# Weight slabs split ahead of time, and filling steps dealt out by another table

## The chip, the cores and the metric

The kernel runs on one NeuronCore of a Trainium2 chip. Its engines are named as in the profile: PE (matrix multiplication; PEld is its loading of weights), DVE (VectorE), ACT (ScalarE), POOL (GpSimd) and SP, which only issues transfers. Each engine takes its instructions in a fixed order. The metric is the device time of one execution in microseconds (us); the time before is the median of three runs.

## The reference

A two-layer decoder over one sequence of 1024 tokens with 1024 features. Layer 0 mixes tokens by differential attention, layer 1 by forgetting attention, and each is followed by a gated MLP; a layer norm stands after each of the four parts. Only layer 1's attention is touched:

```python
def forgetting_attention(x, w_in, b_f, w_o):
    q, k, v, f_logit = jnp.split(x @ w_in, [H * d, 2 * H * d, 3 * H * d], axis=-1)
    ...
    log_f = jax.nn.log_sigmoid((f_logit + b_f).astype(jnp.float32))
    c = jnp.cumsum(log_f, axis=1).transpose(0, 2, 1)
    ...
        s = (jnp.einsum('bhqd,bhkd->bhqk', qb, k).astype(jnp.float32) * scale
             + cb[..., :, None] - c[..., None, :])
        p = masked_softmax(s, causal_mask(start, Q_BLOCK, S)).astype(v.dtype)
        o = jnp.einsum('bhqk,bhkd->bqhd', p, v)
    ...
    return sweep_query_blocks(block, S, Q_BLOCK) @ w_o
```

There are 16 heads of 64 features.

## The kernel before

**Numbers in two parts.** Every operand of a dense product is split into a high part and a rest (`split`, line 90): ACT copies the source into the high part's tile, rounded, and DVE subtracts that from the source into the low part's tile. A dense product is then three matmuls (`mm3`, line 100): high with high, high with low, low with high. Because all operations go through such helpers, many instructions of the profile have a helper's line: L93 and L95 are the two halves of a split, L104, L109 and L110 the three matmuls.

**Layer 1's attention, in order of time.**

1. `all_values` (line 430) projects all values. It runs 64 slots (two groups of features, four pairs of token tiles, eight tiles of the contraction), each of two `mm3`, six matmuls. The list `at` hangs other work on a slot: transposes of the layer's input, splits of the value weights, the forget gates, and the splits of the first pair's two weight slabs at slots 36 and 42. Results are split and written to DRAM (`vd`).
2. `first_pair` (line 417) projects q (slab 0) and k (slab 1) of the first pair of heads, in two column halves c of 512 tokens, then loads that pair's values (`load_v`) and cumulated gates (`load_c`).
3. The loop over eight pairs of heads in `attention` (line 782). A pair has 16 jobs: head 0 with query tiles 0 to 3, head 1 with the same, head 0 with tiles 4 to 7, head 1 with these. A job (`fox_scores`) forms the scores of 128 queries with all earlier keys (two matmuls a chunk, L591 and L592), their maximum on DVE (L599), the exponential on ACT one job later (L767), and the division by the sum on DVE one job after that (L770, L771). When a group of four jobs is done, `Values` transposes the probabilities on PE two key tiles a job (L1619), splits them from PSUM (L93, L95, tag `pt`, a ring of three tiles) and multiplies them with v one job later (L1645, L1646).

**Filling.** While a pair's jobs run, the next pair's q and k are projected in between, so that PE has work while DVE and ACT do the softmax. This is `project` (line 485): 32 steps of one `mm3` each, eight for k's first half, eight for its second, then q's two. Each group of eight accumulates into one of four PSUM banks (tag `m`), which the transposes and the products with v use too. Step 0 fetches k's slab and step 8 makes q's slab ready; step 24 makes the k slab of the pair after ready, which step 16 fetched. `ahead` (line 339) issues a fetch into one of two staging tiles (`wst`), `ready` (line 344) splits the staged slab into `wh` and `wl` (three buffers each, also used for some of the probabilities).

**The dealing.** How many steps follow each job is set in `attention`: a job has a weight, for layer 1 its number of key tiles plus 2, that is 3, 4, 5, 6, 3, 4, 5, 6, 7, 8, 9, 10, 7, 8, 9, 10, sum 104; after each job, steps are run until the share of steps done is the share of weights passed. The first pair runs 8 steps ahead of its jobs, and the last pair's filling is the output projection. The order in which instructions stand on each engine is laid out from this program order, by priority, when the kernel is built, so neighbours may change places.

**Slabs.** For layer 1, `slabs[3 p]` is the q weight of pair p, `slabs[3 p + 1]` its k weight, each 128 x 1024 numbers of 4 bytes, 512 KB. From 24 on stand the output projection's.

Of the kernel before, what the change touches and what calls it, by code (L numbers as in the profile page):

```python
# [9 lines left out]
F32 = mybir.dt.float32  # L10
F32R = mybir.dt.float32r
# [8 lines left out]
P = 128  # L20
# [3 lines left out]
NP = 8  # L24
# [14 lines left out]
LAG, VLAG, W_C = 1, 0, 2  # L39
# [14 lines left out]
T_ST, N_R, N_A = 2, 4, 6  # L54
X0_A, X0_B, X1 = 2, 2.5, 13
W_V, FRAC = 1, 0
V_T, V_W, V_LD = 5, 8, 12
TT1 = 3


class Trunk:
# [276 lines left out]

    def ahead(self, i):

        if i < len(self.slabs):
            self.stage[i] = self.fetch(self.slabs[i])

    def ready(self, i):
        if i < len(self.slabs):
            self.w[i] = self.cut(self.stage.pop(i))

    def first_loads(self, pos):
# [68 lines left out]
    def first_pair(self, t):  # L417

        self.all_values()
        for c in range(2):  # L420
            for s in range(2):
                if c:
                    self.ready(4) if s else self.ahead(4)
                ps = self.mbank()
                self.dense(ps, *self.w[s], c)
                self.result(1, s, c, ps, None, t)
        self.load_v(0, t)
        self.load_c(0, t)

    def all_values(self):  # L430

        nc = self.nc
        self.vd = [self.dr.tile([P, KT, 4, 2, P], F32, name=f"vd{g}") for g in range(2)]
        own = lambda: self.qtile(0)
        high, low = [partial(self.wp.tile, [P, 1024], F32R, tag=t, name=t + "v") for t in ("wh", "wl")]
        other = partial(self.tmp, F32R, self.pp, "p")  # L440
        homes = ((own,) * 4 + (high, low) * 2, (other,) * 4 + (high,) + (own,) * 3)
        w, stage = {}, {}

        def cut(g, kt):
            if kt % 2 == 0:
                stage[g] = self.fetch(self.i["wv1"][g, kt // 2])
            hl = homes[g][kt]()
            w[g, kt] = hl[:, :512], hl[:, 512:]
            self.split(*w[g, kt], stage[g][:, kt % 2 * 512:kt % 2 * 512 + 512])

        at = [[] for _ in range(64)]
        for kt in range(KT):
            cut(0, kt)
            at[V_T + 2 * kt].append(partial(self.transposes, self.acc, 1, (kt,), True))
            at[V_W + 3 * kt].append(partial(cut, 1, kt))
        at[25] += [partial(self.gate_logits, 1), self.forget_gates]
        for s in range(2):
            at[36 + 6 * s].append(lambda s=s: self.w.update({s: self.weight(self.slabs[s])}))
        at[48].append(self.forget_sums)
        n = 0  # L460
        for g in range(2):
            for t0 in range(0, 8, 2):
                ps = [self.mbank() for _ in range(2)]
                for kt in range(KT):
                    for fn in at[n]:
                        fn()
                    n += 1
                    for j in range(2):
                        self.mm3(ps[j], *self.x_lhs(kt, t0 + j), *w[g, kt], kt == 0, kt == KT - 1)
                for j in range(2):  # L470
                    out = self.tmp(F32R)
                    parts = out.rearrange("p (a b d) -> p a b d", a=4, b=4)
                    self.split(parts[:, :, 0::3], parts[:, :, 1:3], ps[j].rearrange("p (a h d) -> p a h d", a=4, h=2))
                    nc.sync.dma_start(self.vd[g][:, t0 + j], out.bitcast(F32).rearrange("p (a h d) -> p a h d", a=4, h=2))

    def x_lhs(self, kt, tt):
        ts = slice(tt % 4 * P, tt % 4 * P + P)
        return self.xh[kt, tt // 4][:, ts], self.xl[kt, tt // 4][:, ts]
# [303 lines left out]
    def attention(self, l):  # L782

        nc = self.nc
        self.od = self.dr.tile([NP, P, 1024], F32, name=f"od{l}")
        tiles = lambda p: [self.qtile((p + l) % 2) for _ in range(7)] + (
            [self.lp.tile([P, 1024], F32R, tag="lg", name=self.nm("kl"))] if l else [])
        self.slabs = [self.i[f"w{l}"][s * NP + p] if s < 3 - l else None for p in range(NP) for s in range(3)]  # L790
        self.slabs += [self.i[f"wo{l}"][k] for k in range(8)]
        self.w, self.stage, self.queue = {}, {}, []
        self.ofs, self.fill = {}, None
        if l == 1:
            for h in range(2):
                for t in self.qz[h]:
                    nc.gpsimd.memset(t[64:66, :].bitcast(F32), 1.0)
            self.gate_logits(0)
        cur = tiles(0)
        self.first_pair(cur) if l else self.first_pair_rotary(cur)  # L800
        live, values = [], []
        for p in range(NP):
            nxt = tiles(p + 1) if p < NP - 1 else None
            if nxt is not None:
                self.fill, n = self.project(l, p + 1, nxt), 32 if l else 48
            else:
                self.fill, n = self.out_early(l), 64
            jobs = (self.diff_jobs if l == 0 else self.fox_jobs)(p, cur)
            done = 0
            if p == 0:  # L810
                for done in range(1, (EARLY if l else EARLY0) + 1):
                    self.step()
            total, acc, base = sum(j[0] + 1 + W_C for j in jobs) - (W_V * 12 if l == 0 else 0), 0, done

            def steps(goal):
                nonlocal done
                while done < min(goal - 0.5, n):
                    self.step()
                    done += 1

            for job in jobs:
                live, values = self.tick(live, values, job)
                w = job[0] + 1 + W_C - (W_V * self.coming(values) if l == 0 else 0)
                acc += w
                goal = base + (n - base) * acc / total
                steps(done + (goal - done) * FRAC)
                values = self.tock(values)
                steps(goal)
            while done < n:
                self.step()  # L830
                done += 1
            next(self.fill, None)
            cur = nxt
        self.fill, n = self.out_late(l), 12
        while live or values:
            live, values = self.tick(live, values, None)
            values = self.tock(values)
            for _ in range(min(n, T_ST)):
                self.step()
                n -= 1  # L840
        for _ in range(n):
            self.step()
        self.load_o(7, self.ofs[NP - 1])
        for _ in self.fill:
            self.pulse()
# [848 lines left out]
class Norm:  # L1694
# [19 lines left out]
    def tiles(self, t0, n=1):  # L1714
        k = self.k
        return (t0, [k.small(tag="nm") for _ in range(n)],
                *[k.small(n, f"n{j}", 4 if n == 1 else 1) for j in range(3)])
# [120 lines left out]
```

## Time and profile before

| what | us |
|---|---|
| median of three runs | 2409.92 (2409.3 to 2410.89) |
| the profiled execution | 2413.51 |
| its span, first to last instruction | 2410.8 |
| values of layer 1 projected | about 1192 to 1280 |
| first pair projected | 1280 to 1302 |
| seven pairs with a filling projection | about 1302 to 1620 |
| one pair in the middle | 50.0 |

Durations come from the profiled execution. In a table by stretches of time, "x" is a count of instructions, PEclk the share of full TensorE clock that was granted, then the mean busy share of the 16 DMA engines and the rate in GB/s. A line of the waits names who waited, for whose instruction, us in total, times, and the longest. A timeline line has start, duration, engine, line, operation, and what it writes and reads. Groups of instructions end in "xcount | busy us, mean ns", and DMA lines in count, size and median us from issue to landing.

### The profile page before, as it was taken

How to read it: one execution, taken by the hardware profiler on the slowest of the kernel's cores; microseconds unless marked ns; L12 is line 12 of the kernel's file. 1: busy time of each engine (PE TensorE's matmuls, PEld its weight loads, DVE VectorE, ACT ScalarE, POOL GpSimd, SP SyncE). 2: the span in 40 equal slices, each digit the busy share in tenths (PEclk: the TensorE clock that was granted, in tenths of full speed). 3: DMA queues.
4: the chain of work that ended last, by engine and by line, in shares of the span. 5: the costliest groups of instructions: out<-in, count | busy, mean ns of one | idle time of the engine just before them, and what ended most of it. 6: DMA issues, size and time to landing. Idle time of an engine off the chain costs nothing. (4 is left out here: it accounts for less than half of the span.)

```text
span 2410.8 us, 33786 instructions
## 1 busy us (share of the span) xinstructions
PE 2389.0 (99%) x11627; PEld 1981.5 (82%) x11627; DVE 1905.6 (79%) x3740; ACT 1259.6 (52%) x2381; POOL 199.8 (8%) x396
## 2 busy tenths in 40 slices
PE   9999999999999999999999999999999999999998
PEld 7888888778888888888888888888888888888886
DVE  5888888889987877777833888889899887777768
ACT  4656666556544445544523555666465444445434
POOL 2111111010000110100100100101010001110000
PEclk9999999999999999999999999999999999999999
DMA  6223333521433557866334333345223335559672
GB/s 185 67 78 96 88 86 108 188 90 61 171 118 120 128 135 209 250 224 212 131 136 136 86 82 88 91 113 178 90 81 139 123 118 131 132 144 314 197 227 104
DMA packets 159275, 329.02 MB, mean 136 GB/s; under 512 B 21328, under 2 KB 44880, under 8 KB 159104
## 3 DMA queue, kind: packets, MB, share of 16 engines
q1 hardware_dynamic: 147904, 305.83, 39.1%
q0 software_dynamic: 10912, 20.98, 5.4%
q8 instruction: 91, 1.49, 0.2%
q14 instruction: 80, 0.66, 0.1%
q10 hardware_dynamic: 288, 0.07, 0.0%
HBM read 202.60 MB, written 90.64 MB: 122 GB/s over the span
## 5 line engine op out<-in xcount | busy, mean ns | idle before, releaser
L104 PE MATMUL m<-xh,wh 128*128 128x512 f32 x640 | 260.2, 407 | 0.1
L104 PE MATMUL m<-xh,wo 128*128 128x512 f32 x656 | 255.7, 390 | 0.0
L109 PE MATMUL m<-xl,wo 128*128 128x512 f32 x656 | 255.6, 390 | 0.0
L110 PE MATMUL m<-xh,wo 128*128 128x512 f32 x656 | 255.2, 389 | 0.0
L110 PE MATMUL m<-xh,wl 128*128 128x512 f32 x640 | 252.3, 394 | 0.0
L109 PE MATMUL m<-xl,wh 128*128 128x512 f32 x640 | 251.0, 392 | 0.0
L599 DVE CUSTOM_DVE_ANT_0 s<-s,mask 128x384 f32<-128x384 f32 (+7 forms) x256 | 194.2, 760 | 26.6 <-PE s L592 25.8
L93 ACT ACTIVATE wo<-wg 128x512 fp32r<-128x512 f32 (+1 forms) x168 | 102.2, 609 | 168.6 <-PE m L110 141.7
L93 ACT ACTIVATE pt<-m 128x512 fp32r<-128x512 f32 (+3 forms) x285 | 131.5, 491 | 101.6 <-PE m L1619 96.1
L95 DVE TENSOR_TENSOR pt<-m,pt 128x512 fp32r<-128x512 f32 (+3 forms) x285 | 153.8, 557 | 26.3 <-ACT pt L93 24.5
L583 POOL CAST qz<-q 64x128 fp32r<-64x128 f32 x256 | 94.7, 373 | 820.0 <-PE s L592 710.8
L93 ACT ACTIVATE wo<-t 128x512 fp32r<-128x512 f32 x132 | 83.5, 632 | 126.8 <-PE m L110 81.0
L110 PEld LDWEIGHTS m<-xh,wo 128*128 128x128 f32 x656 | 123.1, 188 | 25.6
L104 PEld LDWEIGHTS m<-xh,wo 128*128 128x128 f32 x656 | 123.3, 188 | 24.9 <-ACT p L1312 0.2
L109 PEld LDWEIGHTS m<-xl,wo 128*128 128x128 f32 x656 | 123.3, 188 | 24.3
L110 PEld LDWEIGHTS m<-xh,wl 128*128 128x128 f32 x640 | 120.2, 188 | 26.0 <-DVE wl L95 0.8
L104 PEld LDWEIGHTS m<-xh,wh 128*128 128x128 f32 x640 | 120.5, 188 | 21.1 <-DVE pt L95 1.2
L591 PE MATMUL s<-q,q 128*128 128x512 f32 (+4 forms) x384 | 134.8, 353 | 1.8 <-ACT wst L637 1.6
L95 DVE TENSOR_TENSOR wo<-wg,wo 128x512 fp32r<-128x512 f32 (+1 forms) x168 | 110.5, 659 | 32.8 <-ACT wo L93 32.1
L109 PEld LDWEIGHTS m<-xl,wh 128*128 128x128 f32 x640 | 120.8, 189 | 18.9
L95 DVE TENSOR_TENSOR wo<-t,wo 128x512 fp32r<-128x512 f32 x132 | 90.7, 688 | 48.7 <-ACT wo L93 48.5
L104 PE MATMUL m<-q,wo 128*128 128x512 f32 x328 | 128.6, 392 | 0.0
(416 smaller groups left out, 6528.8 us busy)
## 6 DMA issues: line engine op xcount, KB each, us to landing
wb<-in_wd SPq DMA_DIRECT2D x142, 256.0 KB, 5.2
t<-in_wi SPq DMA_DIRECT2D x44, 512.0 KB, 4.5
ha<-ad SPq DMA_DIRECT2D x86, 256.0 KB, 5.3
wg<-in_wi SPq DMA_DIRECT2D x42, 512.0 KB, 4.0
ad<-t SPq DMA_DIRECT2D x40, 512.0 KB, 2.6
wst<-in_w SPq DMA_DIRECT2D x38, 512.0 KB, 3.6
ha<-sd SPq DMA_DIRECT2D x66, 256.0 KB, 3.9
q<-q SPq DMA_DIRECT2D x128, 128.0 KB, 2.3
```

The source lines that it names most:

```text
L93: self.high = nc.scalar.activation(hi, src, AF.Copy, scale=1.0 if scale is None else scale)
L95: self.low = nc.vector.tensor_tensor(lo, src, hi.bitcast(F32), op=ALU.subtract)
L104: last = mm(out, wh, xh, start=start, stop=False)
L109: mm(out, wh, xl, start=False, stop=False)
L110: mm(out, wl, xh, start=False, stop=stop)
L583: nc.gpsimd.tensor_copy(qz[r:r + 64, :], q[r:r + 64, qt * P:qt * P + P])
L591: nc.tensor.matmul(sb[:, ks], q[:, qt * P:qt * P + P], kd[:, ks], start=True, stop=False)
L599: self.nc.vector.tensor_tensor_reduce(sb[:, :ln], sb[:, :ln], self.mask[:, 1024 - ln:], 1.0, BIG, ALU.add, ALU.min, mn)
```

## The change

Twelve slabs, q and k of the pairs 2 to 7, are fetched and split during the projection of the values: the fetch of number m hangs on slot 3 + 5 m, and the split (`keep`) three slots later. `keep` splits into two tiles of the ring `pt` and writes both parts to DRAM through POOL's queue. `ahead` then does nothing for such a slab, and `ready` loads the two parts from DRAM into `wh` and `wl` instead of splitting. The first pair is projected k first, with both halves, and the loads of gates and values stand between k and q; the slots of its two slabs are swapped. For layer 1's pairs 0 to 6 the weights of the 16 jobs are taken from SHARE, sum 321.

```diff
+SHARE = (13, 27, 21, 9, 6, 19, 20, 8, 32, 30, 14, 15, 39, 37, 15, 16)
+V_T, V_W, V_LD, W_P = 5, 8, 12, 3
...
     def ahead(self, i):
-        if i < len(self.slabs):
+        if i < len(self.slabs) and i not in self.parts:
             self.stage[i] = self.fetch(self.slabs[i])
     def ready(self, i):
-        if i < len(self.slabs):
+        if i in self.parts:
+            self.w[i] = [self.wp.tile([P, 1024], F32R, tag=t, name=self.nm(t)) for t in ("wh", "wl")]
+            for t, part in zip(self.w[i], self.parts.pop(i)):
+                self.nc.sync.dma_start(t.bitcast(F32), part)
+        elif i < len(self.slabs):
             self.w[i] = self.cut(self.stage.pop(i))
...
     def first_pair(self, t):
         self.all_values()
-        for c in range(2):
-            for s in range(2):
-                if c:
-                    self.ready(4) if s else self.ahead(4)
+        for s in (1, 0):
+            for c in range(2):
+                if s == 0:
+                    self.ready(4) if c else self.ahead(4)
                 ps = self.mbank()
                 self.dense(ps, *self.w[s], c)
                 self.result(1, s, c, ps, None, t)
-        self.load_v(0, t)
-        self.load_c(0, t)
+            if s:
+                self.load_c(0, t)
+                self.load_v(0, t)
...
         for s in range(2):
-            at[36 + 6 * s].append(lambda s=s: self.w.update({s: self.weight(self.slabs[s])}))
+            at[42 - 6 * s].append(lambda s=s: self.w.update({s: self.weight(self.slabs[s])}))
         at[48].append(self.forget_sums)
+        for m in range(2 * NP - 4):
+            i = 3 * (2 + m // 2) + (1 - m % 2)
+            at[W_P + 5 * m].append(partial(self.ahead, i))
+            at[W_P + 5 * m + 3].append(partial(self.keep, i))
...
+    def keep(self, i):
+        hl = [self.tt.tile([P, 1024], F32R, tag="pt", name=self.nm("wk")) for _ in range(2)]
+        self.split(*hl, self.stage.pop(i))
+        self.parts[i] = [self.dr.tile([P, 1024], F32, name=self.nm("wk")) for _ in range(2)]
+        for part, t in zip(self.parts[i], hl):
+            self.nc.gpsimd.dma_start(part, t.bitcast(F32))
...
-            total, acc, base = sum(j[0] + 1 + W_C for j in jobs) - (W_V * 12 if l == 0 else 0), 0, done
+            even = l == 1 and p < NP - 1
+            total, acc, base = sum(SHARE) if even else sum(j[0] + 1 + W_C for j in jobs) - (W_V * 12 if l == 0 else 0), 0, done
...
-            for job in jobs:
+            for m, job in enumerate(jobs):
                 live, values = self.tick(live, values, job)
-                w = job[0] + 1 + W_C - (W_V * self.coming(values) if l == 0 else 0)
+                w = SHARE[m] if even else job[0] + 1 + W_C - (W_V * self.coming(values) if l == 0 else 0)
                 acc += w
                 goal = base + (n - base) * acc / total
```

More of the change, by code (lines that the diff above doesn't have):

```diff
@@ L56 @@
 W_V, FRAC = 1, 0
-V_T, V_W, V_LD = 5, 8, 12
+SHARE = (13, 27, 21, 9, 6, 19, 20, 8, 32, 30, 14, 15, 39, 37, 15, 16)
+V_T, V_W, V_LD, W_P = 5, 8, 12, 3
 TT1 = 3
@@ L791, in attention @@
         self.slabs += [self.i[f"wo{l}"][k] for k in range(8)]
-        self.w, self.stage, self.queue = {}, {}, []
+        self.w, self.stage, self.parts, self.queue = {}, {}, {}, []
         self.ofs, self.fill = {}, None
```

## The prediction

> **What bounds the kernel now.** I read the page first, then the table by stretches of time (the windows), the waits, and the timeline where they pointed.
>
> ```profile
> PE 2389.0 (99%) x11627; PEld 1981.5 (82%) x11627; DVE 1905.6 (79%) x3740; ACT 1259.6 (52%) x2381; POOL 199.8 (8%) x396
> core 0: us, PE busy (x) PEld busy (x) DVE busy (x) ACT busy (x) POOL busy (x), PEclk, DMA share, GB/s
> 1192.00:1280.00 88.00, 88.00 (x405) 71.37 (x403) 30.01 (x54) 20.68 (x36) 0.38 (x1) 1.00 0.40 141
> 1280.00:1302.00 22.00, 22.00 (x99) 18.22 (x98) 4.53 (x6) 3.73 (x6) 1.05 (x4) 1.00 0.57 172
> 1302.00:1320.00 18.00, 17.29 (x85) 13.61 (x84) 9.54 (x32) 8.12 (x23) 2.26 (x8) 1.00 0.66 175
> 1393.67:1443.67 50.00, 49.67 (x265) 40.74 (x264) 40.70 (x100) 29.42 (x66) 4.78 (x16) 1.00 0.33 91
> ```
>
> PE is the bound, at full clock (PEclk 1.00). The rows after the page's are the stages that the change touches, all in layer 1: the projection of the values (88 us), the first pair's projection (22 us), the start of the pairs, and one whole pair, which takes 50.00 us and repeats. VectorE (DVE) has 30.01 of 88 us of work in the values stage and 40.70 of 50 in a pair: the first has room, the second little.
>
> "PE busy" does not tell whether PE waits, because a matmul's bar covers its pipeline. I take the distance from start to start:
>
> ```profile
> 1291.78 0.39 PE L104 MATMUL m<-xh,wh 128*128 128x512 f32 x1
> 1292.01 0.39 PE L109 MATMUL m<-xl,wh 128*128 128x512 f32 x1
> 1292.24 0.39 PE L110 MATMUL m<-xh,wl 128*128 128x512 f32 x1
> 1292.46 0.39 PE L104 MATMUL m<-xh,wh 128*128 128x512 f32 x1
> ```
>
> One filling step (three matmuls) takes 1292.46 - 1291.78 = 0.68 us where nothing is waited for. Now the waits of PE's weight loads, first over all the pairs with a filling projection (1302 to 1620 us), then in the two halves of one pair:
>
> ```profile
> PEld m L1646 <- DVE pt L95: 9.7, 30, 0.4
> PEld m L1645 <- ACT pt L93: 7.3, 24, 0.8
> PEld m L1645 <- issue: 1.5, 4, 0.4
> ...
> PEld m L1646 <- DVE pt L95: 1.7, 5, 0.4
> PEld m L1645 <- ACT pt L93: 1.1, 4, 0.4
> PEld m L1645 <- issue: 0.4, 1, 0.4
> ...
> PEld m L104 <- DVE q L95: 0.2, 1, 0.2
> ```
>
> So 18.5 us are waited in seven pairs, nearly all of it by the products (L1645, L1646) for the split of transposed probabilities on ACT and DVE. In one pair it is 3.2 us in the first half (rows four to six) and 0.2 in the second (the last row). The halves are jobs 0 to 8 and jobs 9 to 15; they begin at these score matmuls:
>
> ```profile
> 1393.67 0.22 PE L591 MATMUL s<-q,q 128*128 128x128 f32 x1
> 1418.21 0.40 PE L591 MATMUL s<-q,q 128*128 128x512 f32 x1
> ...
> 1393.67:1418.21 24.54, 24.21 (x131) 19.05 (x130) 20.68 (x59) 15.20 (x38) 2.59 (x9) 1.00 0.28 80
> 1418.21:1443.67 25.46, 25.46 (x135) 21.69 (x134) 20.02 (x41) 14.22 (x28) 2.19 (x7) 1.00 0.39 101
> ...
> 1393.67:1418.21 24.54, 5.25 (x13) 2.46 (x13) 1.00 0.28 80
> 1418.21:1443.67 25.46, 7.85 (x19) 3.58 (x19) 1.00 0.39 101
> ```
>
> The last two rows count line L104, one a step: 13 steps in the first half, 19 in the second. DVE has as much to do in both (20.68, 20.02 us), in many more instructions (59 against 41), so PE runs out of cover in the first half and never in the second.
>
> **The change part by part.**
>
> *The dealing.* With the old weights the jobs 0 to 8 get 43 of 104 shares of 32 steps, 13.2, as counted. With SHARE they get 155 of 321, 15.5. So 2.2 steps, 2.2 x 0.68 = 1.5 us of PE work, move from the half without waits to the half with them. Inside the half it is uneven: jobs 1, 2, 5, 6 and 8 gain 4.1 steps together, jobs 3, 4 and 7 fall from 4.6 to 2.3.
>
> *The splits that leave the pairs.*
>
> ```profile
> L95 DVE TENSOR_TENSOR wl<-wst,wh 128x1024 fp32r<-128x1024 f32 x8 | 9.6, 1206 | 0.0
> L93 ACT ACTIVATE wh<-wst 128x1024 fp32r<-128x1024 f32 x8 | 8.5, 1059 | 1.0 <-PE m L109 1.0
> ...
> 1397.51 1.20 DVE L95 TENSOR_TENSOR wl<-wst,wh 128x1024 fp32r<-128x1024 f32 x1
> 1426.30 1.21 DVE L95 TENSOR_TENSOR wl<-wst,wh 128x1024 fp32r<-128x1024 f32 x1
> ```
>
> Each pair has two, 1.21 us on DVE and 1.06 on ACT each. The one at 1426.30 lies where PE never waits: worth nothing. The one at 1397.51 stands in DVE's queue between splits that PE waits for: up to 1.2 us.
>
> Steps and split together could close 1.5 + 1.2 = 2.7 us of the 3.2 in a pair. The ends are 3.2 (all) and -1.0 (the steps taken from jobs 3, 4 and 7, 2.3 x 0.68 = 1.6 us, open new waits, 0.6 gained elsewhere). I take 2.0, nearer to the sum, as not every step lands in a wait. It counts for the pairs 1 to 6: 6 x 2.0 = 12. Pair 0 keeps its split (slab 3) and has 24 steps left after its 8 early ones, of which 1.65 move: 1.0.
>
> In place of each split two loads of 512 KB go to SP's queue, one more than before (4 instead of 2 a pair, some 21 GB/s on 91). They land in about 4 us (the row wst below) and are used 8 steps later, over 10 us: hidden. They now wait in SP's queue for a free buffer of wh and wl, as the split waited on ACT; of the three, one holds the weights in use, one the slab before, one a job's probabilities that are transposed by job 6 (or 10), so one is free at steps 8 and 24. Behind them stand the moves of q and k and the loads of v, none due sooner.
>
> *The values stage gets 12 fetches, 12 splits and 24 writes.* DVE gains 12 x 1.21 = 14.5 us on 30.01 of 88, ACT 12.7 on 20.68: hidden by PE's 88 us. The transfers are the dear part:
>
> ```profile
> wst<-in_w SPq DMA_DIRECT2D x38, 512.0 KB, 3.6
> ad<-t POOLq DMA_DIRECT2D x4, 512.0 KB, 7.2
> L1362 POOL DMA_DIRECT2D ad<-t x4: 559/562/572, 953.7 to 2206.5; - x4
> ```
>
> POOL issues 24 x 0.56 = 13 us, and has only 0.38 us else in this stage. A new split is due every 5 slots, 5 x 6 x 0.227 = 6.8 us. Its two tiles come from a ring of three (tag pt), of which the gate weights hold one until slot 25. Split and write take 1.06 + 1.21 + 7.2 = 9.5 us by these rows: 2.7 too long, for the four splits up to there 10.8 us, of which transposes due 4 slots later (5.4 us) hide half. And the bytes: 88 us x 141 GB/s + 36 x 0.524 MB = 31.3 MB, at the stage's own rate (141 / 0.40 = 352 GB/s) 89 us: the transfers just fill the stage. By the rate of the start of the pairs (175 / 0.66 = 265 GB/s) it would be 118 us, 30 too many. The ends are 0 (PE never waits here now, so nothing can be gained) and 30; I take 3, near the stage's own rate.
>
> By the Trainium skill, "DMA: Bandwidth & Descriptors", section "Anatomy of one DMA", a write from this queue takes about 2.0 us plus its bytes at 436 GB/s, an estimated 3.2 us here, and the cost would be 0. The row's 7.2 us, from a busier stage, speaks against it; no row shows such a write in this stage.
>
> *The first pair's order.*
>
> ```profile
> 1307.42 0.22 PE L591 MATMUL s<-q,q 128*128 128x128 f32 x1
> 1307.97 0.40 SPq L750 DMA_DIRECT2D q<-cd  x1
> 1311.10 0.40 PE L592 MATMUL s<-q,qz 66*128 66x128 f32 x2
> ```
>
> Job 0's second score matmul waits for the forget sums' load, issued at 1307.97 behind k's moves. The change issues it after k, half a projection earlier, so DVE can start up to 3.1 us sooner. PE meanwhile does filling steps, so this is worth 0 to 2; I take 0.5.
>
> *Sum.* 12 + 1.0 + 0.5 - 3 = 10.5 us less. The profiled execution took 2413.51 us (span 2410.8 and 2.7 around it), the median of the runs 2409.92, 3.6 less: 2403.0 for such an execution, 2399.4 for the median. I say 2399.
>
> **The rivals.**
>
> *The waits only move (same).* Steps need a PSUM bank as well as a place:
>
> ```profile
> 1409.22 0.39 PE L104 MATMUL m<-xh,wh 128*128 128x512 f32 x1
> 1414.36 0.68 DVE L95 TENSOR_TENSOR q<-m,q 128x512 fp32r<-128x512 f32 x1
> 1414.43 0.40 PE L104 MATMUL m<-xh,wh 128*128 128x512 f32 x1
> ```
>
> For 5 us no step runs, and the next group of eight starts beside DVE's emptying of the last one's bank. With SHARE this border moves from job 6 to job 5, one with transposes too. If the steps dealt to the first half so run late, a pair gains 0.6 (half of the split): 6 x 0.6 + 0.5 - 3 = 1 less, 2409. For it: the row at 1409.22; against it: 13 steps were run where 13.2 were dealt.
>
> A second way to no gain: the pairs are as full as the values stage by PE's loads, 40.74 / 50 = 0.81 against 71.37 / 88 = 0.81. Then 3 us are lost: 2413. The waits, 3.4 us in a pair and none in the values stage, contradict it. That reading is a rule of the Trainium skill, "Perfetto Trace Analysis", section "Identifying the Most-Contended Engine": judge PE by the share of its weight loads, not of its matmuls. The trace disagrees here: a load takes its time whether the matmul behind it streams 512 columns or 128.
>
> *The transfers bind the values stage (slower).* Place: the ring of three tiles, behind which ACT, in order, holds the transposes and the emptying of banks. At 265 GB/s the stage grows by 30 us: 2409.9 - 13.5 + 30 = 2426. It decides the sign below 31.3 MB / (88 + 13.5) us = 308 GB/s. For it: the nearest two stages run near 300 GB/s and below (172 / 0.57, 175 / 0.66); against it: those load v in small pieces, this stage does not.
>
> *Nearly all waits go.* 6 x 3.2 + 1.1 + 2 - 0 = 22 less: 2388. For it: the second half shows that no waits are possible at the same DVE load.
>
> The change may also fail to do what it says: the last new split hangs at slot 61 of 64, and what slips runs in the first pair, where DVE has 4.53 of 22 us. That costs nothing.
>
> **How the numbers follow.** The forecast (2391 to 2405) has 0.58, the moved waits 0.20, the full loads 0.02, the transfers 0.14 (0.04 of it ending within 0.2%), nearly all waits gone 0.06. Within 0.2% (4.8 us, about what a measurement of this kernel can tell from no change): 0.20 + 0.02 + 0.04, less 0.03 of the moved waits that end faster, 0.23. Slower: 0.14 - 0.04 = 0.10. Faster: 0.58 + 0.06 + 0.03 = 0.67. The range 2390 to 2413 leaves out the slow transfers and half of the best case.
>
> **What would show it.** Right: a middle pair's period falls from 50.0 to about 48; the waits for pt in its first half from 3.2 to about 1.2 us; 15 or 16 steps in jobs 0 to 8; the values stage still about 88 us with a DMA share near 1. Wrong: ACT waiting for POOL's writes in the values stage and PE for transposes; or new waits in jobs 3, 4 and 7, or after job 9.

## The result and the profile after

The changed kernel is 0.8% slower: 2430.87 us in the median of five runs (2426.77 to 2431.88) against 2410.71 (2409.3 to 2412.86) for the kernel before on the same chip, a ratio of 1.0079 [1.0065, 1.0093] (here and below, the 95% interval in brackets). The forecast was 2399 in a range that ended at 2413. The profiled execution of the changed kernel took 2431.88 us with a span of 2430.1, that of before 2410.8.

Where the 19.3 us come from is read from the first score matmul of each pair (L609 now, L591 before), and from the table by stretches of time. The timeline of the changed kernel has these starts of pair 0 and of two neighbouring pairs in the middle:

```profile
1327.60 0.22 PE L609 MATMUL s<-q,q 128*128 128x128 f32 x1
...
1413.73 0.30 PE L609 MATMUL s<-q,q 128*128 128x128 f32 x1
...
1463.38 0.31 PE L609 MATMUL s<-q,q 128*128 128x128 f32 x1
```

Pair 0 starts at 1327.6 instead of 1307.4, 20.2 us late. A pair in the middle takes 1463.38 - 1413.73 = 49.65 us instead of 50.0. The first two pairs together take 0.1 less and what follows the start of pair 7 takes 1.1 us more (768.3 against 767.2). So 20.2 are lost ahead of the pairs, 2.0 won in all the pairs, and 1.1 lost behind them. The last is no more than the stretch varies: in the runs below it takes 766 to 771 us. The windows of the changed kernel show the place:

```profile
core 0: us, PE busy (x) PEld busy (x) DVE busy (x) ACT busy (x) POOL busy (x), PEclk, DMA share, GB/s
1192.00:1290.00 98.00, 83.45 (x357) 65.64 (x357) 41.15 (x64) 30.51 (x46) 12.88 (x24) 0.91 0.84 308
...
1200.00:1210.00 10.00, 10.00 (x52) 8.24 (x51) 4.41 (x7) 2.26 (x4) 1.06 (x2) 1.00 1.01 362
1210.00:1220.00 10.00, 4.69 (x16) 3.60 (x15) 4.82 (x7) 4.32 (x8) 1.06 (x2) 0.66 0.67 234
...
1230.00:1240.00 10.00, 6.49 (x22) 3.21 (x22) 5.74 (x8) 3.64 (x6) 2.13 (x4) 0.83 0.88 319
1270.00:1280.00 10.00, 4.28 (x14) 2.95 (x13) 4.72 (x8) 2.34 (x4) 1.60 (x3) 0.73 1.02 376
```

Before, PE was busy for all 88 us of the values stage. Now it has three holes, of 5.7, 3.9 and 5.9 us from one matmul's start to the next. DVE's work in the stage is no more than was foreseen (41.15 us; 30.01 + 14.5 were), and the mean rate of 308 GB/s is about what the prediction had called enough. So neither an engine nor the bytes as such are the answer. The waits of the same stretch (1190 to 1330 us) name it:

```profile
ACT wk L94 <- DMA wst<-in_w: 29.1, 8, 5.3
DVE wk L96 <- DMA wk<-wk: 23.7, 7, 7.5
...
ACT wk L94 <- DMA wk<-wk: 11.1, 3, 4.7
...
PEld m L105 <- DVE t L96: 6.2, 2, 5.9
...
PEld s L1085 <- DVE xl L96: 5.7, 1, 5.7
...
PEld m L724 <- DVE t L96: 3.9, 1, 3.9
```

The last three lines are PE's holes. In each PE waits for DVE: for the split of a transposed input tile (xl) and twice for the emptying of a bank (t). DVE stood, for up to 7.5 us at a time, before the split of a slab (wk) whose tile an earlier slab's write had not yet left. In the first hole that is the whole chain, as the timeline shows:

```profile
1206.74 0.53 POOL L492 DMA_DIRECT2D wk<-wk  x1 [0.96 <-DVE wk L96]
...
1210.07 1.06 ACT L94 ACTIVATE wk<-wst 128x1024 fp32r<-128x1024 f32 x1 [4.69 <-DMA wk<-wk]
...
1214.49 1.22 DVE L96 TENSOR_TENSOR wk<-wst,wk 128x1024 fp32r<-128x1024 f32 x1 [7.55 <-DMA wk<-wk]
1215.63 0.68 DVE L96 TENSOR_TENSOR xl<-s,xh 128x512 fp32r<-128x512 f32 x1
...
1216.37 0.90 PE L1085 MATMUL s<-ident,acc 128*128 128x128 f32 x3 [5.31 <-DVE xl L96]
1217.14 0.78 PE L105 MATMUL m<-q,xh 128*128 128x512 f32 x1
1217.71 0.63 PE L110 MATMUL m<-q,xh 128*128 128x512 f32 x1
1218.14 0.63 PE L111 MATMUL m<-q,xl 128*128 128x512 f32 x1
```

POOL issues the write of a low part at 1206.74. ACT's half of the next slab runs at 1210.07, but DVE's half waits for that write until 1214.49. Behind it, in order, stands the split xl, and behind that PE's next transposes, at 1216.37. The last two rows show a second price: two matmuls of 512 columns start 0.43 us apart, where the prediction's rows had 0.23. The granted clock has fallen (0.66 in that window). There are some 21 such matmuls behind the three holes, 21 x 0.2 = 4.2 us. The holes beyond the normal pace are 14.8 us; together 19.0 of the 20.2.

The other two holes have more than one cause. At the second, the gate logits, DVE's slab split waited for a write until 1230.15, but the split behind it waited for ACT, and ACT until 1231.05 for a fetch of value weights: by these times either alone would have made most of it. At the third, writes held both engines. ACT empties a bank (its half of t) right behind a slab's split that waited 2.79 us, and DVE does so behind its own half of that split:

```profile
1272.73 1.06 ACT L94 ACTIVATE wk<-wst 128x1024 fp32r<-128x1024 f32 x1 [2.79 <-DMA wk<-wk]
1273.69 1.07 ACT L94 ACTIVATE t<-m 128x512 fp32r<-128x512 f32 x2
1275.66 1.23 DVE L96 TENSOR_TENSOR wk<-wst,wk 128x1024 fp32r<-128x1024 f32 x1 [3.76 <-ACT t L94]
1276.80 0.68 DVE L96 TENSOR_TENSOR t<-m,t 128x512 fp32r<-128x512 f32 x1
...
1277.54 0.79 PE L105 MATMUL m<-p,xh 128*128 128x512 f32 x1 [5.50 <-DVE t L96]
```

The third row's wait is put down to ACT, which was done by 1274.8; the write that had to leave the tile, issued at 1269.37, landed at 1275.1.

How long the writes took is told by the view of the tile wk in the changed kernel (from issue to landing, shortest, median, longest):

```profile
DMA to landing us min/median/max: 2.9/5.9/7.7
```

### The profile page after: what moved, and what is told of

The parts are those of the page before. It is cut to its first block, busy times and chain, and to the rows that moved or that the text cites. A ratio compares the mean times of both kernels' runs of the same rounds, so it can differ in the third digit from the quotient of the medians.

```text
span 2430.1 us, 33886 instructions
## 1 busy us (share of the span) xinstructions
PE 2390.6 (98%) x11627; PEld 1985.1 (82%) x11627; DVE 1910.1 (79%) x3740; ACT 1259.2 (52%) x2381; POOL 211.9 (9%) x420
## 5 line engine op out<-in xcount | busy, mean ns | idle before, releaser
L609 PE MATMUL s<-q,q 128*128 128x512 f32 (+4 forms) x384 | 133.9, 350 | 3.2 <-ACT wst L655 1.4
L110 PEld LDWEIGHTS m<-xl,wh 128*128 128x128 f32 x640 | 120.8, 189 | 18.5
```

The costliest lines, as they stand in the source:

```text
L110: mm(out, wh, xl, start=False, stop=False)
L609: nc.tensor.matmul(sb[:, ks], q[:, qt * P:qt * P + P], kd[:, ks], start=True, stop=False)
```

## The experiments

All were timed beside the kernel before. "Waits in a pair" are worked out from the trace: over five middle pairs (2 to 6) the distances between matmul starts beyond the usual pace of the same shape (0.2266 us for 512 columns), in mean. Before it is 3.36 us a pair, with the changed kernel 2.99. The sums hang on the pace that is taken for the short matmuls; the differences do not.

The start of pair 0 also carries what happened ahead of the stage, where no run changes anything. The first matmul of the gate logits stands there, the same in all. In the timelines of before, the changed kernel, e4 and e10:

```profile
1181.52 0.40 PE L706 MATMUL m<-xh,wf 128*48 128x512 f32 x1
...
1181.01 0.40 PE L724 MATMUL m<-xh,wf 128*48 128x512 f32 x1
...
1183.50 0.40 PE L721 MATMUL m<-xh,wf 128*48 128x512 f32 x1
...
1180.00 0.40 PE L723 MATMUL m<-xh,wf 128*48 128x512 f32 x1
```

From it to pair 0 are 125.9 us before and 146.6 in the changed kernel. What a run has beyond 125.9 is called lost ahead of pair 0 below: 20.7 in the changed kernel.

**One part at a time.** The change has three: the dealing (SHARE), the early splits, and the order of the first pair.

The dealing alone (e1). Left out of the changed kernel are the early splits and the new order:

```diff
-        for m in range(2 * NP - 4):
-            i = 3 * (2 + m // 2) + (1 - m % 2)
-            at[W_P + 5 * m].append(partial(self.ahead, i))
-            at[W_P + 5 * m + 3].append(partial(self.keep, i))
```

> The new dealing alone: no slab is split ahead, the first pair keeps its old order. If the dealing closes part of the waits in the first half of a pair, as the prediction had it (1.5 us of PE work moved there, seven pairs): a pair takes 48.5 to 49 us and the whole 2400 to 2404. If the waits only move to other jobs: a pair takes 49.6 to 50.2 us and the whole 2407 to 2412.

Measured: 1.0002 [0.9993, 1.001], pairs of 49.7 us, waits in a pair 3.07: the second branch. The dealing alone is worth 0.3 us a pair, nothing that a run can tell.

Early splits and new order without the dealing (e2):

```diff
-            even = l == 1 and p < NP - 1
+            even = False
```

> The changed kernel with the old weights of the jobs. If the loss lies in the values stage and its transfers: job 0 of the first pair starts at about 1327 us as in the changed kernel (1307 before) and the whole takes 2427 to 2433. If the dealing is what costs: 2408 to 2414. By the pairs' period it shows what the early splits are worth by themselves: 49 us if the split in DVE's queue cost up to 1.2 us, 50 if nothing.

Measured: 1.0040 [1.0029, 1.0052]. The three holes are there (5.1, 4.1, 5.3 us), pair 0 starts at 1325.1, and 19.0 us are lost ahead of it. But the pairs are shorter than with the whole change. Two starts in the middle, from its timeline:

```profile
1459.49 0.22 PE L609 MATMUL s<-q,q 128*128 128x128 f32 x1
...
1508.29 0.22 PE L609 MATMUL s<-q,q 128*128 128x128 f32 x1
```

That is 48.80 us, 1.2 less than before: the whole 1.2 of one split on DVE, as the prediction had it. SHARE on top of it takes 0.8 of them back. The order alone (e3: all of the dealing and the splits left out):

> The kernel before with the first pair projected k first, the loads of gates and values between, and the slots of the two slabs swapped. If the earlier load of the gates starts the jobs' DVE work sooner: 0 to 2 us less, 2408 to 2410. If the order delays q: job 0 starts later than 1307 us and the whole takes over 2412.

Measured: 0.9994 [0.9986, 1.0003]. Pair 0 is 1.2 us shorter, and the pair behind it gives 0.8 of that back.

**The writes.** In e4 the slabs are fetched and split early as in the changed kernel, but not written; the pairs split them again themselves, so their parts come from there:

```diff
-        self.parts[i] = [self.dr.tile([P, 1024], F32, name=self.nm("wk")) for _ in range(2)]
-        for part, t in zip(self.parts[i], hl):
-            self.nc.gpsimd.dma_start(part, t.bitcast(F32))
```

> The changed kernel in which the twelve slabs are fetched and split in the values stage but not written to DRAM; the pairs fetch and split them again as before. So the fetches, ACT's and DVE's added work stay, the 24 writes and what waits for them go. If the writes are the cause (their tiles come free too late, or the transfers are full): PE's three holes in the values stage go, job 0 starts at 1307 to 1310 us, the whole takes 2405 to 2412. If the splits themselves crowd ACT and DVE, or the fetches crowd the staging tiles: holes of several us stay and the whole takes over 2420.

Measured: 1.0009 [1.0, 1.0017]. That lies between the two branches. One hole of 3.4 us is left, at the gate logits, and pair 0 starts at 1314.2, with 4.8 us lost ahead of it. So of the 20.7 us the writes account for 15.9; 4.8 remain with fetches and splits alone. There ACT, in order, still waits for the slabs' fetches:

```profile
ACT wk L94 <- DMA wst<-in_w: 24.9, 10, 4.9
```

Is it the bytes, the queue, or the tiles that a write holds? Three runs try it. In e5 the same writes go to SP's queue:

```diff
-            self.nc.gpsimd.dma_start(part, t.bitcast(F32))
+            self.nc.sync.dma_start(part, t.bitcast(F32))
```

> The changed kernel, with the 24 writes of split slabs issued by SP's queue instead of POOL's. Theory A (a write from POOL's queue takes 5.9 to 7.7 us to land and holds its tile of the ring of three for so long; DVE, in order, stands before the next split): writes that land sooner shrink the holes of PE in the values stage from 14.8 us to under 8, and job 0 of pair 0 starts at 1312 to 1320 us instead of 1327.6; ratio 1.002 to 1.005. Theory B (the bytes fill the transfers whatever the queue): the holes stay within 3 us of 14.8, job 0 at 1325 or later, ratio 1.007 or more. A third way: SP, which waits in order for each split, now also holds up the fetches behind the writes, and the holes grow.

Measured: 1.0031 [1.0019, 1.0043], as theory A had it. Windows and waits (1190 to 1310) of this run:

```profile
1192.00:1281.09 89.09, 88.45 (x406) 71.44 (x406) 41.32 (x64) 30.50 (x46) 0.62 (x1) 1.00 0.86 312
```

```profile
ACT wk L94 <- DMA wst<-in_w: 26.7, 8, 4.9
```

The stage takes 89.1 us up to the first pair's first weight load, 1.1 more than before, with PE at full clock and at the same 312 GB/s at which the changed kernel has its holes. Bytes as such are out. ACT waits as long for the fetches as before (26.7 against 29.1), and PE doesn't mind; what has gone is DVE's wait for writes (all waits for the writes of wk: 4.2 us in this run by the tile's view, 34.8 in the changed kernel). The timeline shows how soon a write lands here:

```profile
1209.13 1.59 SPq L492 DMA_DIRECT2D wk<-wk  x2
...
1211.92 1.06 ACT L94 ACTIVATE wk<-wst 128x1024 fp32r<-128x1024 f32 x1 [1.35 <-DMA wk<-wk]
...
1213.43 1.23 DVE L96 TENSOR_TENSOR wk<-wst,wk 128x1024 fp32r<-128x1024 f32 x1 [1.28 <-DMA wk<-wk]
```

The first of the two writes, issued at 1209.13, has left its tile by 1211.92, in 2.8 us. By the landings in the trace, the 24 writes take 2.6 to 5.8 us, 3.0 in the median. The price of this version is elsewhere, as the third way had it: SP comes late to the fetch of slab 4, PE has a hole of 4.6 us in the first pair, and pair 0 starts at 1315.1, with 7.4 us lost ahead of it.

In e6 the ring is relieved instead; the high part of a q slab gets a tile of its own:

```diff
-        hl = [self.tt.tile([P, 1024], F32R, tag="pt", name=self.nm("wk")) for _ in range(2)]
+        pt = lambda: self.tt.tile([P, 1024], F32R, tag="pt", name=self.nm("wk"))
+        of = lambda: self.tp.tile([P, 1024], F32R, tag="of", name=self.nm("wk"), bufs=1)
+        hl = [pt() if i % 3 else of(), pt()]
```

> The changed kernel, with the high part of every q slab split into a tile of its own tag, so that the ring of three is asked for three tiles by two slabs instead of four; bytes, queue and splits as in the changed kernel. Theory A (the ring binds): the holes shrink from 14.8 us to 4 to 9, job 0 of pair 0 starts at 1314 to 1322 us, ratio 1.002 to 1.006. Theory B (bytes): no less than 13 us of holes, job 0 at 1325 to 1329, ratio 1.007 to 1.009. If only the first hole goes and the later two stay, the staging tiles are next in line.

Measured: 1.0074 [1.0061, 1.0087], holes of 5.7, 3.7 and 3.8 us. The ratio is theory B's, though e5 has ruled out its cause, the bytes. The ring's size alone is not it either. The waits (1190 to 1310) show where they went:

```profile
ACT wk L94 <- DMA wst<-in_w: 44.1, 12, 8.1
```

29.1 us became 44.1: with another tile the writes are no sooner out (6.6 us in the median, by the same view of wk), and the next split waits for its fetch instead. What is long is each transfer itself, while POOL's and SP's are on their way together.

That left open whether POOL's queue is slow as such, or whether any second queue would be. In e12 the high part is written by ACT's queue, the low part by SP's:

```diff
-        for part, t in zip(self.parts[i], hl):
-            self.nc.gpsimd.dma_start(part, t.bitcast(F32))
+        for q, part, t in zip((self.nc.scalar, self.nc.sync), self.parts[i], hl):
+            q.dma_start(part, t.bitcast(F32))
```

> The changed kernel with all twelve slabs; the high part of each is written by ACT's queue right behind its split, the low part by SP's. Theory A (it is POOL's queue that lands late: 5.9 us in the median, up to 7.7): ACT's writes go out beside SP's fetches as POOL's did and yet land in under 4 us; the holes of the values stage go as with SP's queue (under 3 us in all), ratio 1.000 to 1.004. Theory B (a write that runs beside the fetches of another queue lands late, whichever queue it is; on SP's alone it stood in line with them): ACT's writes land in 5 us or more, holes of 6 us or more in the values stage, ratio 1.004 to 1.008. In both the issue takes ACT's own time.

Measured: 1.0026 [1.0017, 1.0036], inside A's ratio, but with holes of 7.0 us in all, as B had it, and pair 0 at 1316.7. Two of ACT's writes and who waited for them, from the timeline:

```profile
1206.58 0.33 ACTq L492 DMA_DIRECT2D wk<-wk  x1
1210.56 1.06 ACT L94 ACTIVATE wk<-wst 128x1024 fp32r<-128x1024 f32 x1 [3.01 <-DMA wk<-wk]
...
1261.94 0.33 ACTq L492 DMA_DIRECT2D wk<-wk  x1
1268.37 1.06 ACT L94 ACTIVATE wk<-wst 128x1024 fp32r<-128x1024 f32 x1 [5.47 <-DMA wk<-wk]
```

They land in 4.0 and 6.4 us, and ACT's twelve in 4.8 in the median (2.7 to 7.0). So with all twelve slabs a write lands in 3.0 us in the median where SP's queue sends writes and fetches alike, in 4.8 on ACT's queue beside SP's, and in 5.9 on POOL's. The sharing explains a part of the lateness; whether POOL's queue adds the rest isn't settled, as no run has it alone.

**Fewer splits, and later ones.** Only the q slab's split stands in the half of a pair where PE waits; the k slab's split, at step 24, stands in the other. From here on only the six q slabs are split early, with the old weights and the new order. First one every ten slots (e7):

```diff
+        for m in range(NP - 2):
+            i = 3 * (2 + m)
+            at[W_P + 10 * m].append(partial(self.ahead, i))
+            at[W_P + 10 * m + 3].append(partial(self.keep, i))
...
+            even = False
```

> Only the six q slabs are split in the values stage (slots 3 to 56, one every ten slots), the k slabs are split in the pairs as before; steps dealt by the old weights; first pair in the new order. If what the splits gained in the pairs came from the q slab alone (its split stood in the first half, the k slab's in the second where nothing waits), the pairs take 48.8 us as with all twelve. Theory A (ring): a split every 13.6 us leaves each write time to land, the holes go to under 4 us, job 0 at 1307 to 1313, ratio 0.997 to 1.000. Theory B (bytes, now half): the same here. If both slabs mattered: pairs 49.4.

Measured: 1.0008 [0.9999, 1.0017]. The pairs take 48.9 us (mean of five), so the q slab alone brings all of the gain. Both theories missed the values stage. It still has a hole, of 6.4 us at the gate logits, and pair 0 starts at 1316.0, with 9.1 us lost ahead of it: half the bytes, but the split at slot 26 still falls between the gate logits and what they need. No write is waited for there; ACT waits 4.96 us for value weights and 1.33 for the slab. Next the same six from slot 27 on, every six slots (e8, W_P = 27 and 6 in place of 10):

> As the run with six slabs, but the fetches start at slot 27, after the value weights' splits, the transposes and the gate logits, one every six slots up to the end of the stage. What is queued behind a split on DVE is then only the emptying of a bank every eight slots: no holes expected, job 0 at 1307 to 1309, pairs 48.8, ratio 0.996 to 0.998, the fastest of all so far. If a split every six slots (8.2 us) still waits for the ring (write 5.9 to 7.7 us and split 2.3), the stage loses 2 to 6 us at the emptying of banks, ratio 0.998 to 1.000.

Measured: 0.9992 [0.9983, 1.0001] over eleven runs that go from 2406.5 to 2416.0. Pair 0 starts at 1308.3, with 2.2 us lost ahead of it: PE still waits 1.9 us behind a slab's split, now at the forget sums. Then at slots that keep away from the other work (e9):

```diff
+        for m, n in enumerate((27, 31, 38, 43, 51, 56)):
+            at[n].append(partial(self.ahead, 3 * (2 + m)))
+            at[n + 3].append(partial(self.keep, 3 * (2 + m)))
```

> The six q slabs, fetched at slots 27, 31, 38, 43, 51 and 56 and split three slots later, so that none falls on the slab weights (36, 42) or on the forget sums (48); writes by POOL's queue. In the run with six late slabs PE waited 1.9 us at the forget sums, behind two splits that waited for writes. Theory: that hole goes, job 0 of pair 0 at 1306 to 1308 us, pairs 48.8, ratio 0.996 to 0.998 with a narrower spread. If it is not the place of the splits but POOL's writes as such that cost: same as the run with six late slabs, 0.999.

Measured: 0.9993 [0.9984, 1.0002], pair 0 at 1310.8, and the hole at the forget sums is still there (1.7 us): the ratio is its rival's, and the place was not the cause. With the same slots and SP's queue for the writes (e10):

> As the spaced six, with the writes issued by SP's queue. Theory A (POOL's writes land late, SP's in under 3 us): no wait of ACT or DVE for a write is left in the values stage; job 0 at 1306 to 1308; ratio 0.996 to 0.998, equal to the spaced six or 0.001 below it. Rival: SP, in order, waits for the splits, and the fetch of slab 4 comes late as in the run with all writes on SP's queue (a hole of 4.6 us in the first pair): job 0 at 1310 to 1315, ratio 0.999 to 1.001.

Measured: 0.998 [0.9971, 0.9989], the only arrangement of the splits whose interval lies below 1, though it overlaps those of e8 and e9. From its windows and its timeline:

```profile
1192.00:1280.00 88.00, 88.00 (x403) 71.45 (x402) 38.19 (x62) 27.29 (x42) 0.00 (x0) 1.00 0.70 253
```

```profile
1305.94 0.22 PE L608 MATMUL s<-q,q 128*128 128x128 f32 x1
...
1440.87 0.22 PE L608 MATMUL s<-q,q 128*128 128x128 f32 x1
...
1489.70 0.22 PE L608 MATMUL s<-q,q 128*128 128x128 f32 x1
```

The stage is full again (88.00 of 88 us), nothing is lost ahead of pair 0, and a pair takes 48.83. ACT and DVE still wait 6.7 us for writes, against theory A, but no hole of PE comes of it; the writes land in 4.3 us in the median. Up to pair 7 the execution is 7.4 us ahead (1636.2 against 1643.6), 1.5 of it from ahead of the stage and 5.9 from the pairs; the span is only 3.4 less, since 4.0 are lost behind pair 7's start. Of these 2.5 us are one wait of PE at 1642.7, behind ACT, which waited 3.2 us there. The waits call it "issue", but the trace has the semaphore: ACT's next instruction (L1724) scales the gain of the next layer norm, whose load SP issued at 1634.5; it landed at 1643.2, 8.7 us later, against 5.7 before. The profiled runs of before, of the changed kernel and of e2, e8, e9 and e11 wait there 0.6 us at most. Why this load took so long stays open.

**The dealing again.** Where the waits in a pair lie, in sixteenths of its PE work (us, mean of five pairs, from the matmul starts as above; sixteenths 7 to 9 and 12 to 15 are under 0.2 in all four):

```
sixteenth            1     2     3     4     5     6    10    11    16   all
before             0.62  0.23  0.39 -0.02  0.72  0.72  0.07  0.09  0.05  3.36
dealing alone      1.05  0.01  0.03  0.05  0.58  0.58  0.05  0.08  0.25  3.07
splits, old deal   0.51  0.20  0.05 -0.03  0.31  0.49  0.06  0.05  0.05  2.19
changed kernel     1.01  0.01  0.03  0.03  0.59  0.58  0.05  0.08  0.23  2.99
```

SHARE closes the second and third sixteenth, and opens the border between two pairs: the first goes up by 0.4 to 0.5, the last by 0.2. By the weights jobs 14 and 15 get 31 / 321 of 32 steps, 3.1, instead of 19 / 104 of 32, 5.8. The waits name the border too; these are of the changed kernel (1350 to 1665 us); in the same stretch before had one wait for L767 (L785 now), of 0.4 us, and none for wh:

```profile
PEld m L1665 <- DVE pt L96: 7.6, 21, 0.6
PEld m L1664 <- ACT pt L94: 5.5, 13, 0.6
PEld s L609 <- ACT wh L785: 1.6, 5, 0.3
PEld m L105 <- DVE q L96: 1.0, 6, 0.2
PEld s L609 <- ACT t L785: 0.8, 1, 0.8
```

A score matmul now waits for the exponential that frees its bank (L609 for L785). The last run gives steps back to the border (e11, on top of e10):

```diff
+SHARE = (24, 24, 18, 9, 6, 19, 20, 8, 28, 24, 12, 15, 34, 30, 24, 26)
```

> As the spaced six on SP's queue, with dealt weights again, but other ones: (24, 24, 18, 9, 6, 19, 20, 8, 28, 24, 12, 15, 34, 30, 24, 26). In the changed kernel PE waits 1.0 us in the first sixteenth of a pair's work and 0.2 in the last, against 0.5 and 0.05 with the old weights, where SHARE leaves jobs 14 and 15 with 3.1 steps instead of 5.8; in the second and third sixteenth it waits 0.04 instead of 0.25. Theory (SHARE took the steps that cover the border from one pair to the next): with 5.0 steps in jobs 14 and 15 and 2.4 instead of 1.3 in job 0 the border's 0.7 us go and the gain behind it stays: pairs 48.6 to 48.8, ratio 0.996 to 0.998. Rival (any move of steps to the first half costs, because the next group's start is bound by DVE's emptying of a bank): pairs 49.3 or more.

Measured: 0.9984 [0.9975, 0.9993], pairs between 49.1 and 50.2, waits 3.01 a pair. The border closes as the theory said: 0.58 in the first sixteenth, 0.05 in the last. But the fifth, 0.72 before and 0.58 under SHARE, rises to 0.86, and the tenth and eleventh to 0.33 and 0.24, and the sum is what it was. That is the rival's time (49.3 or more), though not by its reason alone: the waits appear wherever steps are taken away. With the q slab's split still in the pair the sum is 3.4 under the old weights and 3.1 under SHARE; with it gone it is 2.2 under the old ones and 3.0 under either new dealing.

## Why the prediction was wrong

**The bound and its place held.** PE bounds the kernel, and in e10, with nothing in its way, it is busy for all 88 us of the stage again.

**The values stage: the step that failed.** The prediction took 3 us for it, between ends of 0 and 30. It measured 20.2, and 20.7 from the gate logits on. The place and the parts were named: the ring of three, held by the gate weights' tile until slot 25, and the engines' order behind it. Three things in the working were wrong.

- The chain was taken as split and write, 9.5 us against a pitch of 6.8. A slab waits twice in a row, ACT for the fetch (2.4 to 5.3 us at a time) and DVE for the write (up to 7.5). The fetches were counted as bytes and not as a link; without the writes, fetches and splits still cost 4.8 us (e4).
- The excess of 10.8 us was called half hidden by transposes due four slots later, and of the 5.4 left 3 were taken. One late split on DVE holds everything behind it: at the first hole 7.55 us on DVE became 5.31 on PE. And the excess did not end at slot 25: the third hole stands at slot 48, and there the writes hold ACT too.
- A hole costs more than its length, since the matmuls behind it start 0.43 us apart instead of 0.23: 4.2 us in all.

The row that the prediction gave for a write (7.2 us) was right: 5.9 in the median and 7.7 at the longest. The threshold that it worked out was not: "below 308 GB/s" decides nothing, since the stage loses 20 us at 308 in the changed kernel and 1.1 at 312 in e5. The rate says what the engines move, not when one tile comes free.

**The rival that came true** was "the transfers bind the values stage", given 0.14 and 2426 us. Its engines were half right: it had ACT hold the transposes and the emptying of banks; in the trace DVE holds the transposes, and both hold the banks. Its price was close by luck: 30 us at a rate of 265 GB/s, less a gain of 13.5, where the runs have 20.2 at 308 GB/s, less 0.9.

**The pairs: the second step that failed, by its size.** 2.0 us a pair were forecast, 0.37 measured (249.9 to 248.1 us over five pairs).

- The split out of DVE's queue was right: 1.2 forecast, 1.2 measured under the old weights. That only the first of a pair's two splits counts was right too (e7, with the q slab alone).
- The dealing's 1.5 was wrong. The steps did move (15 in jobs 0 to 8 instead of 13), and the waits behind the start of the pair went, as foreseen; the steps came from the border, where the prediction saw none to lose, because it read the waits of the second half (0.2 us) as room. They were small because the steps were there.
- The two were added. Under SHARE the split's removal is worth 0.08 (3.07 to 2.99), under the old weights 1.17.

The low end that the prediction kept, -1.0 a pair, had the right kind of mechanism (steps taken elsewhere open waits) but looked for it in jobs 3, 4 and 7, not at the end. The rival "the waits only move", with 0.6 a pair, came nearest here, by another way than its own: the steps did not run late for want of a bank. Two smaller readings were off: the 18.5 us of waits are of six and a half pairs, as pair 6 ends at 1643.6 and not at 1620, and jobs 1, 2, 5, 6 and 8 gain 4.2 steps, not 4.1.

**The first pair's order** was taken at 0.5; alone it measures 0.9994 [0.9986, 1.0003], nothing that can be told. Pair 0's 1.2 us are mostly given back by pair 1.

**What the sum would have been** with the measured terms: 2.0 for all the pairs, 0 for the order, 20.2 lost ahead of them and 1.1 behind, 2.0 - 20.2 - 1.1 = -19.3 us, as the spans differ.

**The signs that were listed** worked. "ACT waiting for POOL's writes in the values stage and PE for transposes" is what the trace shows (11.1 us on ACT, 23.7 on DVE, 5.7 on PE), and the share of the transfers near 1 (0.84) told nothing.

## What to carry to other kernels

Work that is moved to a stage with idle engines brings its transfers with it: follow one piece through fetch, split and write with the latencies of each, while both queues run, and see what stands behind it in order on each engine; a mean rate or a share of busy time doesn't show this. A half without waits is not a half with room: what covers it may be the very steps that are to be taken from it. Gains of two edits that aim at the same wait must not be added; run each alone.

## What the runs showed of the hardware

A 512 KB write from SBUF to DRAM landed in 2.6 to 5.8 us (median 3.0) where SP's queue sent fetches and writes alike (e5), in 2.7 to 7.0 (4.8) on ACT's queue beside SP's (e12), and in 2.9 to 7.7 (5.9) on POOL's beside SP's (the changed kernel). By the Trainium skill, "DMA: Bandwidth & Descriptors", section "Queues, rings and completion order", each DMA engine takes turns between the queues that have work, a packet at a time. The landings fit this, but no run shows the turns themselves.

A short hole can cost clock. The windows of e9 around its hole of 1.7 us at 1257.9:

```profile
1250.00:1258.00 8.00, 8.00 (x37) 6.50 (x35) 2.28 (x5) 2.76 (x4) 1.30 (x3) 1.00 0.96 331
1258.00:1262.00 4.00, 2.50 (x10) 1.83 (x9) 3.67 (x7) 1.61 (x4) 0.83 (x2) 0.87 0.95 378
1262.00:1266.00 4.00, 4.00 (x14) 3.13 (x14) 0.00 (x0) 0.00 (x0) 0.00 (x0) 0.70 1.01 407
1266.00:1270.00 4.00, 4.00 (x19) 3.33 (x18) 0.00 (x0) 0.00 (x0) 0.00 (x0) 1.00 0.95 373
```

PE runs again by 1260.1, and then 0.70 of the clock is granted from 1262 to 1266, with seven matmuls at 0.43 us; e8, with a hole of 1.9 us, has none. The Trainium skill, "TensorE: Matmul & The Clock Gate", section "HAM oscillation — how this bites in real kernels", gives about 3.4 us of idling as what PE must not reach. The holes of 3.9 us and more agree, with 21 slow matmuls behind three of them; that of e9 was shorter and cost clock all the same. What sets e9 apart from e8 isn't known.
